# A decoder step on eight cores: weight and state loads in aligned 4 KB runs, small loads moved to another DMA queue, the sample tile moved from fourth to third place, and layernorm scaling moved to ScalarE

## The chip, the cores and the metric

The kernel runs on all eight cores of one Trainium2 chip, the same program on each, with no exchange between cores. The metric is the device time of the slowest core, in microseconds (us). Some runs are in a slow state: the cores of one die, in one run of both (tile_fourth, 1132.29 us), show a lower granted TensorE clock, and the time is longer. All comparisons here are between fast runs. The engines are called PE (TensorE), DVE (VectorE), ACT (ScalarE), POOL (GpSimd) and SP (SyncE), as the profile calls them.

## The reference, cut to what matters

One layer is applied to two kinds of tokens. Each core gets one prompt of 2048 tokens (16 tiles of 128) and 16 samples of 8 tokens (one tile of 128). Per tile:

```python
a = rmsnorm(h, norm_mix)
u, vg, q, k, vm, o, zi, zf = split(a @ w_in)          # w_in 1024 x 3080
y_gm = gelu(u) * (W_s @ layernorm(gelu(vg)) + b)      # gMLP, per chunk of 128
hm, state = mlstm(q, k, vm, zi, zf, state)            # matrix memory C, 128 x 128 per head
y_ml = sigmoid(o) * rmsnorm_per_head(hm)              # gain ml_norm
h += concat(y_gm, y_ml) @ w_out                       # 1024 x 1024
h += square(relu(rmsnorm(h) @ w_up)) @ w_down         # 1024 x 4096, 4096 x 1024
h += sigmoid(rmsnorm(h) @ w_ple_gate) * (p @ w_ple_proj)
y = rmsnorm(h)
```

The prompt starts with zero state. The sample tile needs 16 x 4 carried state matrices `sC` (4 MB), and writes 4 MB of new ones.

## The kernel before

The program is generated: it lists all operations with their data dependencies, a static scheduler orders them by assumed costs, and each engine then executes its list **strictly in that order**, waiting on semaphores. An engine whose next operation waits for a load stands still, even if later operations of its list could run.

The work goes in two halves (prompt tiles 0–7 with the sample tile, then tiles 8–15). In each half the mixer runs in groups of two tiles, then the FFN in four quarters, then a tail (stage C) per tile.

There are two DMA queues. In this kernel loads issued on POOL cast float32 to bfloat16 on the way (the page counts a w_up load of 1024 x 512 elements as 1024 KB, two bytes each); all weights go there. Loads issued on SP are not cast (xs, 128 x 1024 elements, counts 512 KB, four bytes each). In the profile, queue q0 (software) is POOL's and q1 (hardware) is SP's. The parts that the change touches:

```python
def load_win(names, **kw):                      # 512 of w_in's 3080 columns: rows of 2 KB
    v = w_in.rearrange("(k p) n -> p k n", p=128)
    for nm in names:
        dma(WIN[WSLOT[nm]], v[:, :, COLS[nm]:COLS[nm] + 512], eng="pool", **kw)

def consts_b(af):
    dma(OH[:], coh, eng="pool", after=af)       # a table, cast by the DMA
    ...
def load_csb(h, hf, af):                        # sample state, for the mixer
    j0 = hf * 8
    dma(CSB[hf][:, :, 0:128], sC[j0:j0 + 8, h, :, :].rearrange("j d e -> d j e"), eng="pool", after=af)
    ...
def load_q(qd):                                 # one FFN quarter, in four loads with 2 KB or 4 KB rows
    for hf in range(2):
        c0 = qd * 1024 + hf * 512
        dma(wu[:, :, hf * 512:(hf + 1) * 512], w_up_v[:, :, c0:c0 + 512], eng="pool")
    ...
def stage_C(t):                                 # tail of a tile
    dma(PBF[par], t["p"], eng="pool")           # the tile's p, cast by the DMA
    ...
# layernorm of v, in stage_P
ts("dve", vn, vn, mv[:, 0:1], ALU.subtract, rs, ALU.mult)
# the order of the first half
groups = [sg[0:2], sg[2:4], sg[4:6]] + ([sg[8:9]] if len(sg) > 8 else []) + [sg[6:8]]   # sg[8] is the sample tile
```

## Time and profile before

| | before |
|---|---|
| time, median of 3 runs | 1024.67 us (1023.76 to 1024.76) |
| profiled execution, slowest core (core 2) | 1020.3 us |
| mean of the eight cores' spans | 1010.0 us |
| PE busy in it | 895.8 us |
| packets of the casting queue q0 | 54,224 |

The head of the profile page of the kernel before. In part 1 each engine has its busy time, its share of the span and its instructions. In part 2 each character is a fortieth of the span, in tenths of busy time (for PEclk, in tenths of the full clock). Part 3 has packets, megabytes and the share of the 16 DMA engines' time for each queue.

```profile
span 1020.3 us, 17111 instructions; the slowest of 8 cores (1003.6 to 1020.3 us)
## 1 busy us (share of the span) xinstructions
PE 895.8 (88%) x5807; PEld 539.0 (53%) x5875; DVE 581.2 (57%) x1118; ACT 391.8 (38%) x711; POOL 264.4 (26%) x370
...
PE   2578898937999999999997678998899999999994
...
PEclk9798899967999999999999889999999999999997
DMA  9993010996677768065249400003999909000111
...
q0 software_dynamic: 54224, 59.18, 40.9%
q1 hardware_dynamic: 26380, 30.32, 9.8%
```

PE is the bottleneck, and only its gaps can be won: 1020.3 − 895.8 = 124.5 us on this core. The PE row shows where they are: the first slices, two slices around 210, three at 535–610, and the end. The DMA row is at 9 in the first three slices: there the 16 DMA engines are busy 90% of the time or more.

What PE waited for, in all, from the view of waits (total us, number of times, longest):

```profile
PE pb L252 <- DMA AR<-sC: 15.7, 1, 15.7
PE pb L252 <- DMA AR<-w_in: 10.7, 2, 6.7
...
PE pb L252 <- DMA AR<-pp: 3.6, 1, 3.6
```

Two steps of the chain of waits, at 180–262 and at 525–600 (start us, length us, what). `AR<-sC` is one state load and `AR<-pp` one load of a tile's p, both on the casting queue behind weights:

```profile
189.40 1.11 PE pb L252 x16
190.57 27.98 DMA AR<-sC
...
533.38 22.89 DMA AR<-pp
556.27 0.14 issue
556.40 3.85 PE pb L252 x12
```

A state load of 256 KB in bfloat16 (512 KB as float32 in HBM) takes 28 us because it stands in line behind FFN weights: the two w_up loads issued before it on its queue, at 183.3 and 186.0, landed at 204.1 and 215.6, and it at 218.6. One that was issued at 175.7, before them, landed after 6.8 us. A p load of 64 KB (128 KB in HBM) takes 23 us behind mixer weights: the two w_in loads issued at 530.0 and 532.5 landed at 543.5 and 555.9, and it at 556.3. The quickest p load of this profile landed after 2.2 us.

### The profile page before, as it was taken

The numbers are of one execution on the slowest core, as the hardware profiler recorded it, in microseconds if no ns is written. First come the engines' busy times: TensorE is split into PE (matmuls) and PEld (weight loads), VectorE is DVE, ScalarE is ACT, GpSimd is POOL, SyncE is SP. The second block draws the span as 40 slices with busy tenths as digits, with TensorE's granted clock in tenths as the row PEclk, the third lists the DMA queues.
The fourth block names the chain that finished last, engine by engine and source line by source line (L and its number), as shares of the span: only waits on it lengthen the run. The fifth ranks groups of instructions, "written<-read, shape, count | busy, mean of one in ns | idle before, by whom it ended". The sixth has DMA issues, their size and how long they took to land.

```text
span 1020.3 us, 17111 instructions; the slowest of 8 cores (1003.6 to 1020.3 us)
## 1 busy us (share of the span) xinstructions
PE 895.8 (88%) x5807; PEld 539.0 (53%) x5875; DVE 581.2 (57%) x1118; ACT 391.8 (38%) x711; POOL 264.4 (26%) x370
## 2 busy tenths in 40 slices
PE   2578898937999999999997678998899999999994
PEld 2465476624455555555553267576656555565542
DVE  2354878445656774444665537988864444445664
ACT  4245356425311121114544547655532112124543
POOL 3233345443202220011232323545520001001211
PEclk9798899967999999999999889999999999999997
DMA  9993010996677768065249400003999909000111
GB/s 166 183 172 45 12 45 6 109 146 97 104 142 136 177 161 133 1 86 88 86 105 203 121 22 2 1 2 51 138 144 162 161 2 155 11 1 4 68 45 62
DMA packets 80689, 90.59 MB, mean 89 GB/s; under 512 B 13656, under 2 KB 62044, under 8 KB 80604
## 3 DMA queue, kind: packets, MB, share of 16 engines
q0 software_dynamic: 54224, 59.18, 40.9%
q1 hardware_dynamic: 26380, 30.32, 9.8%
q8 instruction: 48, 0.79, 0.3%
q14 instruction: 37, 0.30, 0.1%
HBM read 134.74 MB, written 13.93 MB: 146 GB/s over the span
## 4 chain that ended last, share of the span: by engine, by line
PE 75%; DMA 9%; DVE 6%; issue 5%; ACT 3%; POOL 2%; DVEq 0%; SPq 0%; POOLq 0%; ACTq 0%
PE pb L252 75%; DVE AR L252 3%; DMA AR<-sC 3%; DMA AR<-w_in 3%; DMA AR<-pp 2%; ACT AR L252 2%; POOL SMALL L252 1%; DMA H<-xp 1%; DVE H L252 1%; DVE SMALL L252 1%; DVE ROWX L252 1%; ACT L252 1%; POOL AR L252 0%; DVE ROWR L252 0%; POOL CST L252 0%
## 5 line engine op out<-in xcount | busy, mean ns | idle before, releaser
L252 PE MATMUL pb<-AR 128*128 128x512 bf16 (+4 forms) x4856 | 838.0, 331 | 62.3 <-DVE AR L252 20.9
L252 PEld LDWEIGHTS pb<-AR 128*128 128x128 bf16 x4924 | 470.8, 100 | 393.8 <-issue 86.3
L252 ACT ACTIVATE AR<-pb 128x384 f32<-128x384 f32 (+5 forms) x349 | 175.5, 513 | 476.0 <-PE pb L252 387.7
L252 DVE TENSOR_TENSOR H<-H,pb 128x512 f32<-128x512 f32 x170 | 116.4, 685 | 136.5 <-PE pb L252 136.3
L252 DVE TENSOR_TENSOR AR<-AR 128x384 bf16<-128x384 f32 (+2 forms) x209 | 122.8, 589 | 109.1 <-ACT AR L252 108.3
L252 ACT ACTIVATE AR<-H 128x1024 bf16<-128x1024 f32 x68 | 71.7, 1054 | 54.4 <-PE pb L252 26.9
L252 PE MATMUL pb<-IDB,AR 128*128 128x128 bf16 x578 | 53.5, 237 | 42.6 <-ACT AR L252 28.7
L252 POOL TENSOR_SCALAR SMALL<-SMALL 128x1 f32<-128x1 f32 x85 | 26.3, 310 | 245.4 <-ACT AR L252 201.9
L252 DVE TENSOR_TENSOR AR<-pb,GN 128x1024 bf16<-128x1024 bf16 x51 | 61.6, 1218 | 36.4 <-PE pb L252 36.4
L252 POOL TENSOR_TENSOR SMALL<-SMALL,NEGH 128x1 f32<-128x1 f32 (+1 forms) x102 | 69.3, 681 | 49.8 <-DVE SMALL L252 29.6
L252 PEld LDWEIGHTS pb<-IDB,AR 128*128 128x128 bf16 x578 | 43.0, 107 | 57.7 <-issue 48.9
L252 ACT ACTIVATE AR<-H,SMALL 128x1024 bf16<-128x1024 f32 x51 | 58.1, 1145 | 35.3 <-POOL SMALL L252 34.9
L276 POOL DMA_DIRECT2D AR<-w_up x16 | 15.0, 935 | 132.7 <-PE pb L252 132.3
L252 DVE TENSOR_TENSOR AR<-pb,AR 128x512 f32<-128x512 f32 (+3 forms) x86 | 43.7, 523 | 9.4 <-ACT AR L252 8.4
L252 ACT ACT_TABLE_LOAD x29 | 37.2, 1283 | 16.1 <-PE pb L252 10.2
L252 DVE SCALAR_TENSOR_TENSOR AR<-AR,pb 128x512 f32<-128x512 f32 x34 | 23.2, 684 | 29.6 <-PE pb L252 20.8
L252 ACT ACTIVATE AR<-AR 128x512 f32<-128x512 f32 x34 | 21.3, 629 | 23.8 <-DVE AR L252 17.2
L252 POOL TENSOR_TENSOR AR<-AR,GROW 128x512 bf16<-128x512 f32 (+1 forms) x19 | 25.5, 1341 | 16.5 <-PE pb L252 8.5
L276 POOL DMA_DIRECT2D AR<-w_in x12 | 11.0, 920 | 68.3 <-PE pb L252 64.3
L252 DVE SCALAR_TENSOR_TENSOR AR<-H,SMALL,AR 128x1024 f32<-128x1024 f32 x17 | 22.9, 1346 | 9.1 <-POOL SMALL L252 8.7
L252 ACT ACTIVATE AR<-pb,GSM 128x129 f32<-128x129 f32 x68 | 20.7, 366 | 13.7 <-PE pb L252 13.5
L276 POOL DMA_DIRECT2D AR<-w_down x16 | 12.2, 765 | 51.4 <-PE pb L252 51.3
(101 smaller groups left out, 434.7 us busy)
## 6 DMA issues: line engine op xcount, KB each, us to landing
AR<-w_up POOLq DMA_DIRECT2D x16, 1024.0 KB, 16.0
AR<-w_down POOLq DMA_DIRECT2D x16, 1024.0 KB, 18.9
AR<-w_in POOLq DMA_DIRECT2D x12, 1024.0 KB, 17.5
H<-xp SPq DMA_DIRECT2D x16, 512.0 KB, 4.6
y_p<-AR SPq DMA_DIRECT2D x16, 512.0 KB, 2.9
AR<-w_out POOLq DMA_DIRECT2D x2, 2048.0 KB, 41.8
AR<-sC SPq DMA_DIRECT2D x8, 512.0 KB, 5.0
AR<-w_pg POOLq DMA_DIRECT2D x2, 2048.0 KB, 27.4
```

What stands on the lines that cost most here:

```text
L252: ins = getattr(e, name)(**kw)
L276: lambda e, out=out, in_=in_, sem=sem, kw=kw: e.dma_start(out=out, in_=in_, **kw).then_inc(sem, 16))
```

## The change

The intent, in four items, numbered as in the prediction:

1. The sample tile goes from fourth to third place in the first half, so that two prompt groups follow it and cover its waits; its state loads are prepared a group earlier; the FFN loads wait for the last state load to be issued and landed (`last_c`).
2. The small loads leave the casting queue: p (16 + 1 tiles) and the table OH go by SP in float32, and POOL (p) or DVE (OH) casts them.
3. The weights are laid out on the host so that one row of a load is an aligned 4 KB run, and two column blocks come in one load (u+v, m+o, q+k; one load each for w_out, w_up and w_down of a quarter). The state is laid out as `[head, d, sample, e]`, 4 KB per row in HBM.
4. Layernorm's subtract-and-scale and two gate rows go from DVE to ACT; the gain `ml_norm` is folded into w_out once per half instead of being multiplied into every gate.

The diff, cut to its core; the host code that re-lays the arrays is left out, and so is the scheduler's model of the loads, which was changed with it: it now counts with two queues instead of one, and with rates by the length of the runs. So the order of work changed in more than item 1.

```diff
-        WIN = [WA.bf(8 * 512, k8(8)) for _ in range(6)]
+        WPAIR = [WA.bf(8 * 1024, k8(8)) for _ in range(3)]
+        WLOC = dict(u=(0, 0), v=(0, 512), m=(1, 0), o=(1, 512), q=(2, 0), k=(2, 512), uv=(0, 0), mo=(1, 0), qk=(2, 0))
         def load_win(names, **kw):
-            v = w_in.rearrange("(k p) n -> p k n", p=128)
             for nm in names:
-                dma(WIN[WSLOT[nm]], v[:, :, COLS[nm]:COLS[nm] + 512], eng="pool", **kw)
+                dma(win(nm), WSRC[nm], eng="pool", **kw)
+        def load_wout(af):
+            dma(WOUT, w_out, eng="pool", after=af)
+            for h in range(4):
+                ts("dve", WOUT[:, 4 + h, :], WOUT[:, 4 + h, :], GN[:, G_MLG + h:G_MLG + h + 1], ALU.mult)
...
-            dma(OH[:], coh, eng="pool", after=af)
+            dma(oh, coh.rearrange("p h t -> p (h t)"), after=af)
+            cp("dve", OH[:].rearrange("p h t -> p (h t)"), oh)
...
-                ts("dve", vn, vn, mv[:, 0:1], ALU.subtract, rs, ALU.mult)
+                stt("dve", nm, mv[:, 0:1], -1.0, rs, ALU.mult, ALU.mult)
+                act(vn, vn, AF.Identity, bias=nm, scale=rs)
...
-            for h in range(4):
-                ts("dve", SGT[d2][:, h, 0:n], SGT[d2][:, h, 0:n], 1.0, ALU.add, GN[:, G_MLG + h:G_MLG + h + 1], ALU.mult)
...
-            dma(CSB[hf][:, :, 0:128], sC[j0:j0 + 8, h, :, :].rearrange("j d e -> d j e"), eng="pool", after=af)
+            last_c[:] = [dma(CSB[hf][:, :, 0:128], sC[h, :, j0:j0 + 8, :], eng="pool", after=af)]
...
-            dma(PBF[par], t["p"], eng="pool")
+            dma(PF[par], t["p"])
+            cp("pool", PBF[par], PF[par])
...
-            groups = [sg[0:2], sg[2:4], sg[4:6]] + ([sg[8:9]] if len(sg) > 8 else []) + [sg[6:8]]
+            groups = [sg[0:2], sg[2:4]] + ([sg[8:9]] if len(sg) > 8 else []) + [sg[4:6], sg[6:8]]
...
-                if si == 0 and gi_ == 2:
-                    sample_prep(marks[1])
+                if si == 0 and gi_ == 1:
+                    sample_prep(marks[0])
...
-            load_q(0)
+            load_q(0, last_c if si == 0 else ())
```

## The prediction

> **What bounds it.** TensorE: the page has PE busy 895.8 of 1020.3 us, and the chain of waits is 75% PE, so at most 124 us of PE idleness can be won. The windows view places it (core 2): 29 us in 0–50 (first x and weights), 14 in 50–110, 4 in 110–200, 16 in 200–220, 11 in 220–260, 20 in 540–600, about 13 in 600–760, much of the rest after 970.
>
> **What the change does to those gaps.**
>
> 1. *Sample tile third, FFN loads behind the last state load.* The waits view shows PE waiting 15.7 us once for a state load (sC): issued at 190.6, landed 28.0 us later in the chain, because four FFN weight loads (issued 183–197) share its casting queue; an undisturbed state load lands in 3.7 us. Two groups now follow the sample tile, and the DMA engines are nearly idle at 90–180. I take back 13–15 us of that wait and 3–5 of the 11 after it. State packets still are 256 bytes in SBUF (42–45 ns each): count unchanged.
>
> 2. *pp loads off the casting queue.* In the chain a pp load takes 22.9 us (533–556) behind w_in casts. PE waits 3.6 us for it, and the tail after it (560–593) limps in short waits. It now goes by SP, cast on GpSimd. [...] Worth 4–9 us. The table OH landed 59 us after issue in the same line, at 87 us, and stage M could not begin before 90; it should now land before 50.
>
> 3. *4 KB runs.* Packet records: w_in's 1 KB (SBUF side) packets take 112–125 ns, w_up's 99–101, 2 KB packets 175–217: per byte 10–15% less. It pays only where PE waits for weights, at the start (10.7 us on w_in) and around 540. But o now lands with m in one 4 MB load, some 5 us later; group 1's u and v can fill that. Net 3–7 us in 0–110, with OH.
>
> 4. *Layernorm to ScalarE, gate gain folded into w_out.* DVE loses 17 x 0.63, 36 small multiplies and two row operations a group, about 30 us; it gains 17 x (0.68–0.41), [...] and scalings of w_out: net about -17 us. ACT gains about 18. PE waits on DVE 35 us and on ACT 32, so this nearly cancels: 0–4 us. Risk: DVE works in order, and stands still if the w_out scaling comes up before that load landed.
>
> PE busy stays at 880–896.
>
> **Sum**: -15 to -38, some lost to the new instruction order. I predict **998 us**, 8 in 10 between **980** and **1014**; faster by over 2%: 0.66, within: 0.32, slower: 0.02.
>
> **Right if**: the wait on sC falls below 3 us; pp leaves the chain; OH's landing precedes stage M; packets of the software queue fall from 54,000 to about 38,000, with the 256-byte ones unchanged; DVE busy about 565, ACT about 410; PE idle falls from 124 to about 98 us.
>
> **Wrong if**: the new static order opens gaps elsewhere (DVE waiting for w_out near 70 and 570, PE for mo or qk near 45–55), FFN weights held back behind the state loads arrive late near 200–230, or ACT becomes the late engine in the mixer. Then the gain is under 15 us and the verdict is "same".

(The four items give 16–20, 4–9, 3–7 and 0–4 us, together 23 to 40, of which the forecast expects 15 to 38. The 4–9 us of item 2 are the author's estimate, from the 3.6 us that PE waited for p and the short waits at 560–593. The fused multiply of item 4 did take 0.68 us in the kernel after, where the product before it took 0.41.)

## The result, and the profile after

| | before | after |
|---|---|---|
| median | 1024.22 us (4 runs, 1022.02 to 1024.76) | 1013.12 us of all 4 runs (1008.34, 1012.71, 1013.52 fast, 1149.48 slow) |
| ratio of fast runs, 95% interval | | 0.988 [0.9842, 0.9919] |
| mean of the eight cores' spans, profiled | 1010.0 us | 997.4 us |
| fastest and slowest core, profiled | 1003.6, 1020.3 us | 987.0, 1011.2 us |

Ratios are computed from the mean time of one kernel's fast runs over that of the other's fast runs in the same rounds, so they are not quite the ratio of the medians that are quoted. In the slow run of the kernel after, die 1 had a clock of 0.80 to 0.82.

The change was forecast to win about 27 us, and won 11. The time itself lies inside the forecast range.

The head of the page of the kernel after (its slowest core is core 1):

```profile
span 1011.2 us, 17114 instructions; the slowest of 8 cores (987.0 to 1011.2 us)
...
PE 896.6 (89%) x5875; PEld 535.7 (53%) x5875; DVE 567.6 (56%) x1073; ACT 402.0 (40%) x739; POOL 244.6 (24%) x348
...
PE   3648997898999999999997899897699999999994
...
q0 software_dynamic: 37984, 57.94, 37.1%
q1 hardware_dynamic: 28972, 32.81, 10.9%
```

The mechanical forecasts came true: PE busy unchanged, q0's packets down by 16,240, DVE down by 14 us and ACT up by 10. The dent around 210 in the PE row is gone, the one at 535–610 is down to one slice. But the start did not improve (3648 against 2578 in the first four slices), and there is a new dent at the "76" near 700.

To see this by stretch, I took the view of windows on every core: the length of a stretch less PE's busy time in it, and the mean over the eight cores. (The last stretch ends at each core's own end. Two cores of each profile lack about 70 of their 5,875 matmul records; that is too few to move a stretch much.)

| stretch, us | 0–50 | 50–120 | 120–200 | 200–270 | 270–500 | 500–600 | 600–730 | 730–930 | 930–end | all |
|---|---|---|---|---|---|---|---|---|---|---|
| before | 26.5 | 14.5 | 4.9 | 21.3 | 1.6 | 17.8 | 10.3 | 0.7 | 15.2 | 112.8 |
| after | 25.9 | 15.5 | 7.9 | 6.9 | 2.0 | 14.6 | 12.9 | 0.2 | 16.8 | 102.9 |

So 14.4 us were won at 200–270 (item 1) and 3.2 at 500–600 (item 2). Nothing was won in the first 120 us (items 2 and 3 were to win there), 3 us were lost at 120–200 and 2.6 at 600–730.

What PE waits for, in the kernel after:

```profile
PE pb L252 <- ACT AR L252: 33.7, 12, 10.0
PE pb L252 <- DVE AR L252: 32.1, 27, 6.5
PE pb L252 <- DVE SMALL L252: 16.0, 8, 7.8
PE pb L252 <- DVE ROWX L252: 12.0, 2, 11.5
...
PE pb L252 <- DMA AR<-w_u: 2.6, 1, 2.6
```

The 15.7 us on sC and the 3.6 on pp have left PE's list. In their place are waits on **DVE**: 16.0 on SMALL, the statistics of the norms, and 12.0 on ROWX, the rows of the gates. (This is core 1, and the list before is core 2's. In the mean of the cores PE waited 11.6 us for sC and 2.3 for pp before, and for neither after.) To see why DVE was late, here is its timeline between 40 and 80 us on the same core (start us, length us, instruction, and in brackets how long it stood idle before and what ended that):

```profile
46.43 0.69 DVE L252 TENSOR_TENSOR WM<-AR 128x512 bf16<-128x512 f32 x1 [5.07 <-DMA AR<-c]
...
50.22 1.13 DVE L252 SCALAR_TENSOR_TENSOR SBC<-pb,GN,SBC 128x128 f32<-128x128 f32 x4 [3.03 <-DMA SBC<-gbs]
63.24 0.18 DVE L252 CAST AR<-NCOLS 128x8 bf16<-128x8 f32 x1 [11.89 <-DMA NCOLS<-snT]
```

And here PE's timeline at that point:

```profile
69.28 0.66 PE L252 MATMUL pb<-IDF,ROWX 128*128 128x128 f32 x2 [11.50 <-DVE ROWX L252]
73.01 0.57 PE L252 MATMUL pb<-DCB,ONEF 128*128 128x8 f32 x2 [3.07 <-DVE DCB L252]
```

DVE stands for 11.9 us before a cast of 128 x 8 elements that needs a 32 KB load (snT), and only afterwards computes the gate rows on which PE waits 11.5 us. A tiny load of the sample tile blocks an in-order engine, which blocks PE. The chain of waits of the kernel after (20–110) has another load of the sample tile, its input xs, as its longest step:

```profile
32.70 4.03 SPq L276
36.77 33.85 DMA H<-xs
```

The DMA issues between 0 and 90 us say the same of core 1; the last number is us from issue to landing, that is, until all its data has arrived. First the kernel before:

```profile
H<-xs SPq DMA_DIRECT2D x1, 512.0 KB, 22.1
...
SBC<-gbs SPq DMA_DIRECT2D x1, 256.0 KB, 12.3
```

And the same view of the kernel after:

```profile
H<-xs SPq DMA_DIRECT2D x1, 512.0 KB, 33.9
...
SBC<-gbs SPq DMA_DIRECT2D x1, 256.0 KB, 18.5
```

The same two loads by the same queue take half as long again. In the mean over the cores, for loads issued between 20 and 80 us: xs 18.5 → 30.3 us, gbs 12.5 → 18.5, a prompt tile's xp 15.5 → 30.9, wsT 10.1 → 14.3.

Near 700 the chain shows POOL waiting for a p load, which item 2 had put in its way:

```profile
701.28 12.97 DMA AR<-pp
...
714.28 0.02 POOLq L235
```

### The profile page after: what moved, and what is told of

Its sections match the earlier page's. It is cut to its first block, busy times and chain, and to the rows that moved or that the text cites. A ratio compares the mean times of both kernels' runs of the same rounds, so it can differ in the third digit from the quotient of the medians.

```text
span 1011.2 us, 17114 instructions; the slowest of 8 cores (987.0 to 1011.2 us)
## 1 busy us (share of the span) xinstructions
PE 896.6 (89%) x5875; PEld 535.7 (53%) x5875; DVE 567.6 (56%) x1073; ACT 402.0 (40%) x739; POOL 244.6 (24%) x348
## 4 chain that ended last, share of the span: by engine, by line
PE 72%; DMA 12%; DVE 6%; issue 4%; ACT 2%; POOL 2%; SPq 1%; DVEq 0%; POOLq 0%; ACTq 0%
PE pb L252 72%; DMA AR<-sC 4%; DMA H<-xs 3%; DVE AR L252 3%; ACT AR L252 2%; DMA o_Vs<-AR 2%; DMA H<-xp 1%; POOL SMALL L252 1%; DMA AR<-pp 1%; SPq L276 1%; DVE SMALL L252 1%; DVE H L252 1%; DMA o_Cs<-AR 0%; DVE ROWX L252 0%; DVE R_1 L252 0%
## 5 line engine op out<-in xcount | busy, mean ns | idle before, releaser
L252 PE MATMUL pb<-IDB,AR 128*128 128x128 bf16 x578 | 49.7, 227 | 37.8 <-ACT AR L252 27.4
L252 ACT ACTIVATE AR<-H,SMALL 128x1024 bf16<-128x1024 f32 x51 | 58.2, 1148 | 31.7 <-POOL SMALL L252 31.4
L252 PEld LDWEIGHTS pb<-IDB,AR 128*128 128x128 bf16 x578 | 40.0, 102 | 49.9 <-issue 42.1
L252 DVE SCALAR_TENSOR_TENSOR AR<-AR,pb 128x512 f32<-128x512 f32 (+1 forms) x51 | 34.6, 684 | 35.4 <-PE pb L252 23.9
L276 POOL DMA_DIRECT2D AR<-w_up x8 | 7.5, 934 | 146.5 <-PE pb L252 146.4
L252 DVE TENSOR_TENSOR AR<-pb,AR 128x258 f32<-128x258 f32 (+2 forms) x69 | 36.8, 554 | 5.2 <-PE pb L252 2.7
L252 POOL CAST AR<-AR 128x256 bf16<-128x256 f32 x17 | 8.2, 482 | 109.0 <-PE pb L252 93.2
L252 POOL TENSOR_TENSOR AR<-MSK,GSM 128x512 f32<-128x512 f32 x17 | 17.9, 1053 | 36.6 <-DVE GSM L252 24.5
L252 ACT ACTIVATE AR<-AR 128x512 f32<-128x512 f32 x34 | 21.2, 627 | 13.4 <-DVE AR L252 10.1
L252 DVE SCALAR_TENSOR_TENSOR AR<-AR,DECBS,pb 128x129 f32<-128x129 f32 x64 | 17.6, 344 | 13.9 <-DMA AR<-sC 13.5
```

The lines of the kernel that those rows point to most:

```text
L252: ins = getattr(e, name)(**kw)
L276: lambda e, out=out, in_=in_, sem=sem, kw=kw: e.dma_start(out=out, in_=in_, **kw).then_inc(sem, 16))
```

## The theories

**Theory A: the longer packets of the casting queue starve the SP queue.** Beside the longer packets SP's loads landed later (xs after 30.3 us instead of 18.5, in the mean of the cores), although the casting queue itself moved no slower: in the packet records at 12–70 us, each of which has the size of one run, the casting packets took 116–119 ns (w_in, 1 KB on the SBUF side) before, and 207–215 ns (2 KB) after, by the mean of each core. That the length of the packets is the cause is the theory's assumption; how the engines divide their time between the two queues no record shows. The theory expects that 2 KB runs in HBM, with the order of all work untouched, bring SP's landings back and the time down.

**Rival B: the new order.** The sample tile and its preparation now fall into the saturated start (at 0–50 us the packets' time was 1.00 of that of the 16 DMA engines on core 0 of the kernel after); its small loads are issued there, whatever the packets are. Undoing the early preparation should then bring the start back.

**Rival C: p on POOL.** The gap near 700 comes from loads of p that POOL waits for in order; holding them back until the mixer is over, or casting them in the DMA again, should close it.

**Rival D: big loads complete late.** m and o, or q and k, land together, so what needs one waits for both. Two loads instead of one should help even with 4 KB runs.

**Rival E: ACT is late in the mixer** because of item 4.

## The experiments

All edits are to the kernel after unless it is said otherwise, and all gave correct results. In sample_prep_late, tile_fourth, item1_only, ln_on_vector and halves, and slightly in pp_dma_cast, the scheduler made a new static order with the edit, so what they measure is the edit together with its order. In "ratio" the kernel before is the denominator. "Idle" is PE's, by stretch, as in the table above.

### pp_late and pp_dma_cast: is it p? (Rival C)

In the kernel after, the first loads of p for the second half are issued, and cast on POOL, in the middle of the mixer, long before the tail needs them. pp_late holds each p load back until the FFN's second quarter (qd 1) is done; the order on PE, DVE and ACT stays identical.

```diff
-            dma(PF[par], t["p"])
+            dma(PF[par], t["p"], after=list(hold))     # hold: last operation of FFN quarter qd 1
```

> The changed kernel with one edit: the pp loads of a half wait for the second FFN quarter, so that the GpSimd casts of the second half's first two tiles can't stand in the mixer stage. TensorE, VectorE and ScalarE keep their order of work exactly. Theory (compute engines that work in order now stand still for small loads; GpSimd for pp near 700 us): TensorE's idle time in 690-730, mean of the cores, falls from 7.8 us to 4.5 or less, and the kernel takes 3 to 6 us less than the changed one (about 1008). Rival (the gap near 700 is a VectorE or ScalarE chain of the moved layernorm): idle there stays within 1 us of 7.8 and the time stays at 1013.

pp_dma_cast undoes p's part of item 2.

```diff
-            dma(PF[par], t["p"])
-            cp("pool", PBF[par], PF[par])
+            dma(PBF[par], t["p"], eng="pool")
```

> The changed kernel with its pp part undone: pp is cast by the GpSimd queue's DMA again. Theory: idle in 690-730 falls to about 4 us as in pp_late (no engine waits for a DMA cast until its reader), while idle in 500-600 goes back up from 14.6 to about 17 us; the time stays within 3 us of the changed kernel. Rival (pp placement does not matter at all): both stretches as in the changed kernel, within 1 us.

Measured (before: 1024.32 us): pp_late 1005.68 us, ratio 0.9865 [0.9811, 0.9918]; pp_dma_cast 1012.94 us, 0.9939 [0.9881, 0.9997].

With the cast back in the DMA, the idle time at 500–600 is 17.7 us again (17.8 before, 14.6 after), so p's part of item 2 is worth 3 us there. At 690–730 pp_dma_cast still has 7.9 us of idle (after: 7.8, before: 3.7), and pp_late 5.3. So the gap near 700 is not p's alone: without any p load on SP it is still there, and its chain then goes through many short steps of POOL, DVE and ACT. What else makes it stays open. pp_late is ahead of the kernel after, but the intervals of the ratios overlap; a gain of p's later place isn't established. Rival C explains at most a few us.

### sample_prep_late: is it the early preparation? (Rival B)

```diff
-                if si == 0 and gi_ == 1:
-                    sample_prep(marks[0])
+                if si == 0 and gi_ == 2:
+                    sample_prep(marks[1])
```

> The changed kernel, but the sample tile's small loads (snT, wsT, gbs, first state loads) are prepared one group later, after the second group's gelu. Theory: VectorE no longer waits 6 to 12 us for snT near 51-63 us, and TensorE's idle time in 0-120 falls from 41.4 us (mean of the cores) to 33-37; 4 to 8 us faster than the changed kernel. Rival (the start is bound by when the weights w_qk land, near 70 us, whatever VectorE does): idle in 0-120 stays within 2 us of 41, the time too.

Measured: 1006.43 and 1013.81 us, and two slow runs (1024.15 and 1107.99). The mean span of the cores in the profile was 999.6 us, against 997.4. At 0–120 the idle time was 41.1 us (after: 41.4), and at 120–270 it rose from 14.8 to 18.4. DVE's wait for snT was gone, as expected (7.4 us in the mean of the cores of the kernel after), and xs landed after 21.4 us. But ACT now waited 22.5 us for prompt tiles (xp) instead of 10.0. The start was no better, so undoing the early preparation does not free it; nor does taking away the one wait for snT, as long as another load is late.

### split_2k: the same work in the same order, with 2 KB runs (Theory A)

Each load with 1024 columns is issued as two loads of 512 columns, at the point where it was issued as one; whoever waits for it waits for both. The order on every engine is identical.

```diff
+        parts = [(out, in_)]
+        if eng == "pool" and list(in_.ap)[-1][1] == 1024:
+            parts = [(out[:, :, c:c + 512], in_[:, :, c:c + 512]) for c in (0, 512)]
-        val = self.dma_cnt.get(skey, 0) + 16
+        val = self.dma_cnt.get(skey, 0) + 16 * len(parts)
...
+        for o_, i_ in parts: ... e.dma_start(out=o_, in_=i_, **kw).then_inc(sem, 16)
```

> The changed kernel in exactly the same order of work on every engine, but each weight load of 1024 columns is issued as two of 512, so runs of 2 KB instead of 4 KB. Theory of the prediction (4 KB runs save 10 to 15 % of DMA time where TensorE waits for weights): 3 to 7 us slower, idle in 0-120 up by 3 to 6 us. Rival (no stage waits for weight bandwidth, and half as long packets let the small loads of the other queue through sooner): within 2 us, VectorE's waits for coh and snT shorter by a third or more.

Measured: 997.23 us (fast runs 993.57 to 1001.59, one slow run of 1133.12), ratio 0.978 [0.9713, 0.9846]. One edit that halves the runs gives back 10 us of ratio, 16 by medians. The same lines of the DMA issues on core 1:

```profile
H<-xs SPq DMA_DIRECT2D x1, 512.0 KB, 20.1
...
SBC<-gbs SPq DMA_DIRECT2D x1, 256.0 KB, 12.5
```

And DVE's timeline on that core:

```profile
44.76 1.11 DVE L252 SCALAR_TENSOR_TENSOR SBC<-pb,GN,SBC 128x128 f32<-128x128 f32 x4
46.63 0.92 DVE L252 CAST AR<-NCOLS 128x8 bf16<-128x8 f32 x1 [0.76 <-DMA NCOLS<-snT]
```

The landings are back to 20.1 and 12.5 us, and DVE's wait of 11.89 us before the cast of snT is 0.76. The weights paid for it. Whoever uses a matrix waits for its second half, and that landed later than the single load had: w_mo at 54.8 us of the span instead of 48.7, w_qk at 72.0 instead of 70.2 (means of the cores). PE waited 7.0 us for w_mo, and the kernel was faster all the same.

### split_rows: two loads, but 4 KB runs (Rival D)

The same edit, cut along the rows (k) instead of the columns: twice the instructions, half the size of each, and the runs stay 4 KB.

```diff
-            parts = [(out[:, :, c:c + 512], in_[:, :, c:c + 512]) for c in (0, 512)]
+            parts = [(out[:, c:c + h, :], in_[:, c:c + h, :]) for h in (list(in_.ap)[1][1] // 2,) for c in (0, h)]
```

> Control for split_2k: the same order and also two DMA instructions for each weight load, but halved by rows, so that every run keeps its 4 KB. Theory ([...] long packets starve the small loads): like the changed kernel, 1010 to 1014, VectorE still waits 6 us or more for snT, xs lands in 30 us or more. Rival (two smaller DMA instructions help by themselves, for instance by finer completion): like split_2k, 994 to 1000, with snT waits of 4 us or less.

Measured (before: 1028.9 us): 1012.99 us, 0.9879 [0.9796, 0.9963], that is, as the kernel after. xs landed after 30.6 us in the mean and gbs after 18.5, both as with single loads. What matters is the length of the run, not the size or the number of the loads.

### split_2k_pp_late: both

The edits of split_2k and of pp_late together.

> Both edits that helped: 2 KB runs and pp held back. If the two take time from different waits: 3 to 6 us less than split_2k, 992 to 995. If both cure the same wait near 700 us (pp waiting behind long packets): as split_2k, 996 to 999.

Measured: 995.65 us, 0.9711 [0.9646, 0.9777]: faster. It is no clear step beyond split_2k; the two intervals overlap.

### tile_fourth: item 1 undone

The old place of the sample tile, FFN loads not held, preparation where it was; items 2, 3 and 4 stay.

```diff
-            groups = [sg[0:2], sg[2:4]] + ([sg[8:9]] if len(sg) > 8 else []) + [sg[4:6], sg[6:8]]
+            groups = [sg[0:2], sg[2:4], sg[4:6]] + ([sg[8:9]] if len(sg) > 8 else []) + [sg[6:8]]
...
-            load_q(0, last_c if si == 0 else ())
+            load_q(0)
```

> The changed kernel with item 1 of the prediction undone: sample tile fourth, its preparation one group later, FFN loads not held behind the last state load. Theory: TensorE's idle in 200-270 goes back from 6.9 to 18-22 us (mean of the cores), and the kernel is 9 to 15 us slower than the changed one, about 1024, as before. Rival (the gain came from the new order through other means, the tile's place matters little): idle in 200-270 below 11, time within 4 us of 1013.

Measured: 1018.17 us, 0.9929 [0.9867, 0.9991]; the interval overlaps that of the kernel after. The idle time is 12.6 us at 200–270, not the 18 to 22 that I expected, and 11.2 at 270–500 (after: 2.0): part of the gap came back later. The mean span of the cores is 1009.2 us, against 1010.0 of the kernel before: without item 1 the rest of the change is worth nothing in the mean of the cores.

### item1_only: item 1 alone, on the kernel before

The three edits of item 1 made to the kernel before (group order, `load_q(0, last_c ...)`, preparation a group earlier), with 2 KB runs, p and OH on the casting queue and layernorm on DVE as they were.

> The kernel before with item 1 of the prediction alone: sample tile third, prepared one group earlier, FFN loads held behind the last state load; everything else as before. Prediction's claim: 16 to 20 us faster than before; from tile_fourth's undoing I expect 5 to 14: 1010 to 1019, idle in 200-270 from 21 to 10 or less. Rival (item 1 works only with the new layout and the new rates in the schedule): within 5 us of before.

Measured (before: 1021.13 us): 1005.42 us (1004.39 to 1006.25), 0.9825 [0.9781, 0.9869], which is 1.75% or 18 us, more than the 5 to 14 that I had expected from tile_fourth. PE idles 7.4 us at 200–270 instead of 21.3. PE's waits:

```profile
PE pb L252 <- DMA AR<-w_in: 14.9, 5, 4.8
PE pb L252 <- DMA AR<-pp: 4.6, 1, 4.6
...
PE pb L252 <- DMA AR<-sC: 0.8, 1, 0.8
```

The prediction gave item 1 16 to 20 us. It is right, and **one of the four items alone takes more off the time than all of them together** by medians (1005.4 against 1013.1, on different chips; by the ratios the intervals overlap). They do not overlap with that of changed_again below, the kernel after on the same chip (0.9933 [0.9887, 0.9979]). It was run at another time.

### ln_on_vector: item 4 undone (Rival E)

```diff
-                stt("dve", nm, mv[:, 0:1], -1.0, rs, ALU.mult, ALU.mult)
-                act(vn, vn, AF.Identity, bias=nm, scale=rs)
+                ts("dve", vn, vn, mv[:, 0:1], ALU.subtract, rs, ALU.mult)
...   # the two gate rows likewise back on DVE
```

> The changed kernel with the ScalarE part undone: layernorm scaling and the two small row operations on VectorE again. Prediction's claim: nearly nothing, within 4 us of 1013, most likely 0 to 4 us slower. Rival (ScalarE became the late engine in the mixer and ate the gain): 5 us or more faster, idle in 600-690 and 120-200 down by 3 us or more together.

Measured: 1011.05 us, 0.9878 [0.978, 0.9975]: no difference from the kernel after. Item 4 neither won nor lost, and Rival E falls. (The folding of the gain into w_out was left in.)

### changed_again, split_2k_again, split_mixer, split_ffn: on one chip

The kernel after and split_2k were run again, unedited, with split_2k for the mixer's matrices only (uv, mo, qk, out) and for all others only (FFN and tail).

```diff
-        if eng == "pool" and list(in_.ap)[-1][1] == 1024:
+        if eng == "pool" and list(in_.ap)[-1][1] == 1024 and in_.tensor.name in ("w_uv", "w_mo", "w_qk", "w_out"):
```

> The changed kernel itself, unedited, so that the split kernels stand beside it on one chip: 1010 to 1015, if the earlier comparison across calls was sound.

> split_2k unedited, on the same chip as the changed kernel: 10 to 18 us less than changed_again. If it is within 5 us, the earlier difference was one of chips and the finding falls.

> 2 KB runs only for the mixer's weights (w_uv, w_mo, w_qk, w_out); FFN and gate weights keep 4 KB. Same order of work. Theory (small loads starve beside long packets, at the start above all): this holds the part in 0-120, where idle falls from 41.4 to about 38, so 4 to 8 of the 12 to 16 us. If the gain were in the FFN loads, nothing: 1011 to 1015.

> The complement: 2 KB runs only for w_up, w_down, w_pg, w_pp. Theory: these compete with small loads at the mixer's ends (lnb, pp, and sC in the state update, 12.4 us of VectorE waits), so idle after 120 falls, by 4 to 8 us in all, and idle in 0-120 stays at 41. Both parts should add up to split_2k's gain within 4 us.

Measured (before: 1024.62 us); the last column is the mean over cores of xs's landing:

| | median us | mean of fast runs | ratio, interval | xs landed after |
|---|---|---|---|---|
| changed_again | 1019.64 | 1018.3 | 0.9933 [0.9887, 0.9979] | 31.1 us |
| split_mixer | 1009.88 | 1009.2 | 0.9851 [0.9796, 0.9906] | 23.4 us |
| split_ffn | 1012.06 | 1010.4 | 0.9863 [0.981, 0.9916] | 31.7 us |
| split_2k_again | 1000.45 | 1000.8 | 0.9769 [0.9739, 0.98] | 23.0 us |

changed_again lies above the 1010 to 1015 that I expected: the ratio of the same kernel went from 0.988 to 0.9933. On one chip, then, the 4 KB runs cost 1018.3 − 1000.8 = 17.5 us. Half of it is due to the mixer's matrices (9.1) and half to the others (7.9); the parts add up, but each of them alone has an interval of some 5 us on either side. The start is moved by the mixer's matrices alone, as xs shows.

The cost is uneven over the cores, which matters because the slowest one is the metric. From the view of cores, the fastest and the slowest core of changed_again:

```profile
core 0: 987.4 us, clock 0.959
...
core 7: 1018.1 us, clock 0.947
```

And those of split_2k_again, on the same chip:

```profile
core 4: 986.4 us, clock 0.959
...
core 5: 998.0 us, clock 0.953
```

The fastest cores are alike; with 4 KB runs the others trail by up to 31 us, with 2 KB runs by 12. The other fast runs agree: the slowest core trails the fastest by 22 to 31 us in the three of changed_again, by 10 to 15 in the four of split_2k_again. Which core is slowest changes from run to run (cores 7, 5 and 2 in those of changed_again). In both profiles of the changed kernel the slowest core is the one on which xs landed last (33.9 us on core 1, 35.0 us on core 7 of the second). On the 16 cores of these two profiles xs took 28.1 to 35.0 us, and on the 16 of the two split_2k profiles 20.1 to 25.8.

### one_issue_2k: 2 KB runs with the same number of instructions

In split_2k there are more DMA instructions as well. Here the host lays each weight matrix out in blocks of 512 columns, and one instruction still loads all 1024, now in runs of 2 KB.

```diff
+        if eng == "pool" and list(in_.ap)[-1][1] == 1024:
+            k_ = list(in_.ap)[1][1]
+            in_ = bass.AP(in_.tensor, 0, [[512, 128], [128 * 512, 2 * k_], [1, 512]])
+            out = out.rearrange("p k (c n) -> p (k c) n", c=2)
```

> The cleanest form of the claim: the changed kernel with the same number of DMA instructions and the same order on every engine; only the weights lie in memory so that each load's runs are 2 KB instead of 4 KB. Theory: xs lands in 22-24 us, VectorE waits 3 to 5 us for snT and about 5 for sC, and the kernel gains 12 to 20 us on the changed one, no less than split_2k did (997 to 1000), since GpSimd's issuing time stays as it was. Rival (it was the two instructions, not the runs): 1010 to 1019.

Measured (before: 1026.49 us): 999.73 us, 0.9745 [0.9721, 0.977]: faster. xs landed after 24.3 us in the mean, gbs after 13.3. So neither more instructions nor more completions did it. Two cautions belong here. w_qk landed *later* than with 4 KB runs (49.8 against 44.7 us), and the kernel was nevertheless faster. And TensorE waited more for w_mo in the same profile, 9.2 us in the mean of the cores, against about 2 at most for any weight with 4 KB runs; w_mo landed at 58.1 us instead of 48.7. As in split_2k, what SP's loads gain the casting queue loses.

### split_1k: shorter still

As split_2k, with four pieces of 256 columns.

> The dose: each weight load in four pieces of 256 columns, 1 KB runs, all orders of work unchanged. Theory [...]: xs, which landed in 30-31 us beside 4 KB runs and in 22-23 beside 2 KB runs, lands in 18 or less, and VectorE's snT wait falls below 3 us; but 512-byte packets took 60 ns in the kernel before against 99-101 for 1 KB ones, some 20 % more engine time for the weights, so w_qk and w_out land 5 to 12 us later; the kernel takes 995 to 1012. Rival (2 KB helps for another reason than sharing, such as the layout in memory): xs stays at 22 or above.

Measured (before: 1021.13 us): 1023.72 us, 0.9991 [0.9929, 1.0053]. This was slower than I had expected. The small loads did land soonest of all (xs 17.3 us, gbs 11.2), so the dose still acts: 30.3, 21.9 and 17.3 us for runs of 4, 2 and 1 KB. But another cost grew. From its page:

```profile
span 1021.9 us, 17195 instructions; the slowest of 8 cores (1002.6 to 1021.9 us)
...
PE 897.6 (88%) x5875; PEld 537.5 (53%) x5875; DVE 576.0 (56%) x1073; ACT 401.3 (39%) x739; POOL 314.5 (31%) x429
```

POOL has 81 more instructions than in the kernel after and 314.5 − 244.6 = 69.9 us more of busy time: 0.86 us for each further casting load, in line with POOL's computing. (On core 1 the load instructions alone took 107.5 us of POOL instead of 34.9.) And near 700 they stand in the chain of waits, ahead of POOL's own operations and of the same p load:

```profile
704.73 1.49 POOL AR L280 x2
...
706.51 1.77 POOL AR L280 x2
708.28 2.08 POOL AR L252 x2
...
711.28 12.24 DMA AR<-pp
```

The packets themselves were less efficient too: at 12–70 us 66–69 ns for 512 bytes on the SBUF side, against 114–120 for 1 KB in split_2k. Which of the two costs ate the gain was not separated. Of runs of 4, 2 and 1 KB, 2 KB is the best for this kernel.

### small_first: the same small loads issued earlier, with 4 KB runs

If late small loads are the damage, then issuing the four that DVE waits for (coh, c01, the first gbs, snT) at about 11 us should help without touching the runs. Only the order on SP changes.

```diff
+        for o in order:
+            n_ = o.calls[1].tensor.name if o.dma else ""
+            if n_ in ("snT", "coh", "c01", "gbs") and n_ not in got:
+                got.add(n_); o.after = []; early.append(o)
+            else:
+                rest.append(o)
+        at = [i for i, o in enumerate(rest) if o.dma and o.calls[1].tensor.name == "lng"][0]
+        order = P.order = rest[:at] + early + rest[at:]
```

> The changed kernel with 4 KB runs and all compute orders unchanged; only the SP queue's order is edited: the four small loads that VectorE stood waiting for at the start (coh, c01, the first gbs, snT) are issued at 11 us, before the long weight loads, instead of 26 to 32. Theory: VectorE's 16 us of waits for these four fall below 4, idle in 0-120 falls by 2 to 5 us, and the kernel gains 3 to 8 us on the changed one: about as much as split_mixer. Rival (TensorE at the start is bound by the landing of the weights alone): idle in 0-120 unchanged within 1 us, or higher, since w_u and w_v are held up.

Measured: two fast runs, 1006.5 and 1007.4 us, ratio 0.984 [0.9771, 0.991]; two slow runs (1068.39 and 1124.2). DVE's four waits went to nothing; the idle time at 50–120 fell from 15.5 to 11.6 us. In exchange DVE waited 8.1 us for another small load (gbias), and PE 5.9 us for w_v and 4.1 for w_mo, in the mean of the cores. The mean span is 992.5 us, against 997.4 and 1001.0 in the two profiles of the kernel after. That points the way the theory says; the intervals alone wouldn't prove it. By the ratios it is a third to three fifths of what 2 KB runs give (0.984, between 0.988 or 0.9933 of the kernel after and 0.9769 of split_2k_again). In the mean span of the cores over the fast runs it is most of it: 992.6 us, with changed_again at 1001.4 and split_2k_again at 992.2 on the same chip (the kernels before: 1012.0 and 1014.6). But the cores still spread by 24.1 and 21.5 us in its two fast runs, although xs landed after 18 to 20 us on every core of the profile.

### halves and halves_small_first: a kernel that beats both

In halves, each half of 512 columns is a load of its own for the scheduler: it lands and releases its users by itself (o before m, q before k), and the scheduler builds its order with 2 KB runs and those loads in view.

```diff
             for nm in names:
-                dma(win(nm), WSRC[nm], eng="pool", **kw)
+                src, dst = WSRC[nm], win(nm)
+                halves = (0,) if len(nm) == 1 else (512, 0) if nm == "mo" else (0, 512)
+                for c in halves:
+                    dma(dst[:, :, c:c + 512], src[:, :, c:c + 512], eng="pool", **kw)
...   # likewise for w_out, w_up, w_down, w_pg and w_pp
```

> A candidate: 2 KB runs as in split_2k, but each half a load of its own with its own completion (o before m, then q, then k, w_out and FFN weights in column halves), and the static order made anew with the 2 KB rate. TensorE waited 7 to 10 us for w_mo in split_2k; o alone lands some 5 us earlier. 985 to 1000; if the new order falls badly, up to 1008.

halves_small_first adds the edit of small_first.

> The candidate halves with the four small loads issued first, compute orders unchanged. VectorE's 7 us of waits for snT, coh, c01 and gbs in 0-120 vanish, but w_u and w_v come 1 to 3 us later, as small_first showed: within 5 us of halves, 978 to 986.

Measured: halves (before: 1021.13 us) fast runs of 979.94 to 986.87 us, median of all five 982.51, ratio 0.96 [0.9547, 0.9653]; halves_small_first (before: 1026.49 us) three fast runs of 983.21 to 991.9 us and one slow, median 990.33, 0.9622 [0.9563, 0.9681], which is above the 978 to 986 that I expected. Two lines of the page of halves, to be held against those of the kernel after above:

```profile
span 978.5 us, 17116 instructions; the slowest of 8 cores (964.2 to 978.5 us)
...
PE   2779988989998999999995989996899999999994
```

A slice is a fortieth of the span, some 25 us here: in the second to fourth slices PE is at 7, 7 and 9, where the kernel after has 6, 4 and 8. In the mean of the cores the idle time at 0–120 is 28.3 us (before 41.0, after 41.4), and the clock stays higher (0.970 to 0.976, against 0.952 to 0.961). halves is 4% faster than the kernel before and 3% faster than the change as it was made. Issuing the four small loads earlier adds nothing any more. Whether the step from split_2k to halves (0.978 to 0.96) comes from the separate completions or from the new order isn't settled: both were changed at once.

## Why the prediction was right or wrong, point by point

**What bounds the kernel, and where the gaps are: right.** PE's busy time, in the mean of the cores, stayed within 1.5% in every run (897.2 us before, 884.1 the lowest, in halves), and most of each gain or loss was in PE's gaps.

**Item 1 (16 to 20 us): right.** Alone it gave 18 us (0.9825; 15 in the mean of the cores over the fast runs, 996.8 against 1012.0), and the wait on sC went from 15.7 us to nothing in PE's list. With it, 3 us were lost at 120–200. On the slowest core the chain of waits has a step of 15.5 us there, the write of o_Vs, for which ACT waits; whether that is the loss was not tested.

**Item 2, pp (4 to 9 us): the place was right, the size wrong.** With p off the casting queue the gap at 500–600 shrank by 3.2 us, and pp_dma_cast, with p back on it, gave all of that back. The rest of the term did not come, and 2.6 us were lost at 600–730. POOL now waits for p in order (15.6 us in the mean of the cores), but that this is the reason isn't shown: pp_dma_cast, where POOL has no p to wait for, keeps the gap at 690–730. **The OH sentence was right about the landing and wrong about its worth:** OH's load landed 11.4 us after issue instead of 57.6, and PE's first product with OH, in stage M, came at 71.9 us in the mean of the cores instead of 88.3. But PE idled as much in the first 120 us as before (41.4 against 41.0): the kernel before had presumably filled the time with other work, which had to be done anyway. With 2 KB runs the same product came at 64.5 us (split_2k), in halves at 58.7. So OH no longer held it. What it still waited for in the kernel after came by SP, late: on core 1, ACT stood 4.3 us before its operation on xs at 70.7, and only then wrote the rows of that product (71.8).

**Item 3 (3 to 7 us won at the start): this is the step that failed.** The prediction reads "per byte 10–15% less. It pays only where PE waits for weights, at the start". The packet times were about right: at 12–70 us 207–215 ns for 2 KB on the SBUF side, against 114–120 for 1 KB in split_2k, some 10% less per byte. (The prediction set w_in beside w_up at 99–101 ns. But w_up's depend on the stretch: in the kernel before they took 138 to 158 ns at 180–230 us and 103 to 114 at 300–400.) The sign of the result was not: with the order of work untouched, 4 KB runs cost 17.5 us against aligned 2 KB runs on the same chip, and 10 to 16 us in the other comparison (ratios, medians). The prediction asked what a longer packet does for its own queue, and never what it does to the loads of the other one, though its own item 2 had just moved p and OH there. The runs showed, in its place:

- SP's small loads land later the longer the casting runs are (xs 17.3, 21.9, 30.3 us for 1, 2, 4 KB), and the 16 cores of the two profiles with 4 KB runs and the 16 with split_2k do not even overlap.
- They land late at the moment when three in-order engines need them: DVE (snT, c01, coh, gbs), ACT (xs), POOL (lnb, p). DVE stood 11.9 us before a cast of 128 x 8 elements.
- It is the run length: not the number of loads or of completions (split_rows, one_issue_2k), and not the early preparation of the sample tile (sample_prep_late).
- The start did not hang on the weights alone: one_issue_2k was faster although w_qk landed 5 us later and w_mo 9.

How the DMA engines divide their time between the queues was not shown. The runs show the landing times: with 2 KB runs instead of 4 KB SP's loads landed earlier (xs after 21.9 us instead of 30.3) and the weights later (w_mo at 54.8 us of the span instead of 48.7). One part of the 17.5 us is explained better than the other. At the start one can follow it from a late landing to PE's wait on one core. In the mean over the cores, however, PE's idle time at 0–120 differs only by 2.2 us on this chip (42.5 against 40.3), and their spans by 9.3 (1001.0 against 991.7; over all fast runs 1001.4 and 992.2), in small parts over the later stretches with DMA traffic and in PE's busy time (894.7 against 890.9). The rest of the 17.5 us is in the spread of the cores (31 us against 12): the slowest cores lose more. That the slowest is the one whose xs took longest was so in both profiles, and in those of split_rows and split_ffn, where xs also stood beside 4 KB runs. It is a hint, not a proof, and small_first speaks against it: there xs took 18 to 20 us on every core, and the cores spread by 24 us all the same. So the late small loads may explain the mean; why 4 KB runs spread the cores stays open.

**Item 4 (0 to 4 us): right**, at its lower end. ln_on_vector made no difference.

**The sum.** Item 1 gave its 18 us, p 3 at 500–600, item 4 nothing; the 2 KB version of the same change stands at 0.977 to 0.978 of the kernel before, 22 to 24 us, close to the forecast of 27. The 4 KB runs then take 10 to 17 of it back. The forecast lists "PE idle falls from 124 to about 98 us"; it fell to 114.6 on the slowest core. Its list of what could go wrong named DVE waiting for w_out, PE waiting for mo or qk, and late FFN weights. All were about weights. None was about the small loads.

**The clock.** At 50–120 PE was granted 0.80 on the slowest core of the kernel after, which was busy for 51.0 of these 70 us, and 0.88 on the slowest core of split_2k, busy for 59.5. Two cores do not show what sets the clock; whether a gap at the start costs more than its own length in this way, no run measured.

**What stays open.** What of the gap at 690–730 isn't p's. (At 600–730 as a whole the three profiles with 2 KB runs alone, split_2k, split_2k_again and one_issue_2k, idle 11.4 to 12.0 us, against 12.9 and 14.9 in the two with 4 KB.) Whether the alignment alone, apart from the length of the runs, was worth anything: no run has aligned 2 KB runs against unaligned ones and nothing else changed, and the packet records show no difference: at 12–70 us the 1 KB packets of w_in, whose rows of 12,320 bytes are not aligned, took 116–119 ns (means of the cores), and those of split_2k in the same stretch, which are aligned, 114–120. Whether the gain of halves is that of separate completions or of the new order. And how the runs' length spreads the cores: their spans differed by 24 and 31 us in the two profiles of the changed kernel, and by 10.5 and 11.6 in those of split_2k.

## What to carry to other kernels

In this kernel the length of one DMA queue's runs decided how late the other queue's loads landed while the engines were saturated (xs after 17.3, 21.9 and 30.3 us beside runs of 1, 2 and 4 KB). Before making a bulk queue's runs longer, list which small loads of the other queue are in flight then, and which in-order engine stands still for each. A layout that moves its own bytes 10% faster can lose to the wait for a 32 KB load; measure it with the order of work held fixed, which takes one edit at the place where the DMA is issued. And test a bundle of four ideas one by one: here one of them gave all of the gain, and one had the wrong sign.
